# Attention weights turned by TensorE transposes and multiplied with the values in plain float32

## The chip, the cores and the metric

The kernel runs on one core of a Trainium2 chip. What counts is the time of one execution on the device, in microseconds (us): 3889.59 us is the median of three runs of the kernel before (3884.24 to 3891.26).

## The reference

Two blocks, one after the other, over 512 tokens (and 256 context tokens in the first block) of 1024 features. All weights and activations are float32.

Block 1 has two layers. Each projects its input and mixes it in three ways: a Fourier mix, attention with 8 query heads over 2 key and value heads of 64 features, and a gated linear recurrence ("HGRN") of 4 heads. In layer 0 the 256 context tokens have queries of their own, so there 512 queries meet 768 keys, and 256 queries meet 256 keys; in layer 1 only the 512 queries remain. A gated feed-forward part follows each mix.

Block 2 has a layer of feed-forward, causal attention with 8 heads beside a linear recurrent unit, and feed-forward; then one with a gated convolution between two feed-forward parts.

The attention, cut to what matters:

```python
s = einsum('bkgqd,bksd->bkgqs', q, k) * HEAD_DIM ** -0.5
p = softmax(s, axis=-1)                      # over the keys
out = einsum('bkgqs,bksd->bkgqd', p, v)      # weights with the values
```

In block 2 the scores of keys that come after the query are masked first.

## The kernel before

Activations lie with features on the 128 partitions and tokens along the row. A float32 product that has to be exact is made of several products in a rounded float32 form (`float32r`): each operand is split into a high part (a copy, on ScalarE) and a remainder (a subtraction, on VectorE or GpSimd), and `mm3` (L238 to L246) adds high by high, high by remainder and remainder by high in one bank of PSUM. Nearly all of TensorE's work is `mm3`. Small products, such as sums of squares (L295), go to TensorE as unsplit float32.

The phases run in a row: the opening, mix of layer 0, feed-forward, mix of layer 1, feed-forward, feed-forward of block 2, its causal attention ("moba" in the code), and so on. Inside a mix, Python generators for the projections (`dense`), HGRN, Fourier and attention are emitted side by side by `_weave`, by a cost that each step yields; a scheduler of the framework then puts the instructions of each engine in their final order. Each engine works through its own list strictly in that order. PSUM has 8 banks of 512 floats, handed out by `ps()`: the bank that has been free for longest comes next. On-chip memory is handed out likewise from `arena` (float32) and `rarena` (float32r), with a third piece, `room`, lent to one of them.

One head of attention in a mix of block 1 (L947 to L981): for each tile of 128 queries TensorE makes the scores (L959, two banks for 768 keys), VectorE takes their maximum (L535) and scales it (L540), ScalarE makes the exponentials and their sum (L541), VectorE the inverse of the sum (L542), and VectorE in layer 0 or GpSimd in layer 1 a diagonal matrix of it (L544). When the four query tiles are done, TensorE turns the weights for each block of 128 keys by a product with that diagonal, which transposes and normalizes them (L971). The 128 x 512 result is split: high part on ScalarE (L211), remainder on VectorE (L212). Two products with the values follow (L975, L976), one for each part; their stationary operand holds the high part of the values in 64 columns and the remainder in the other 64. `pv_out` (L548) adds the two halves of the result: ScalarE copies one (L550), VectorE adds the other (L551). In block 2 the same steps are at L1425 (scores), L1427 (mask, added by VectorE in PSUM), L1439, L1446 and L1447; there only the keys up to the query are turned.

`bcast_r` (L264) spreads per-token numbers over the partitions: VectorE repeats a column (L268), and a float32 product with the identity turns it (L270). Every root mean square of the kernel goes through it.

## Time and profile before

| | us |
|---|---|
| median of three runs | 3889.59 |
| lowest and highest of them | 3884.24, 3891.26 |
| span of the profiled execution, first to last instruction | 3885.8 |

For the profiled execution the span is the only time given; the median lies 3.8 us above it.

| stretch, us from the start | what runs | length | TensorE busy | VectorE busy | ScalarE busy |
|---|---|---|---|---|---|
| 268 to 510 | attention of layer 0, with HGRN and Fourier | 242 | 203.61 | 182.55 | 120.29 |
| 1318 to 1496 | attention of layer 1, with HGRN and Fourier | 178 | 158.21 | 118.20 | 90.10 |
| 2384 to 2506 | causal attention of block 2, with projections | 122 | 112.72 | 95.01 | 55.92 |
| 600 to 1100 | feed-forward of layer 0 | 500 | 497.74 | 215.90 | 160.99 |

How to read it: over the whole span TensorE is busy 95% of the time, VectorE 51%, ScalarE 35%. A matmul row in the profile lasts from its first column to the end of its drain, so rows of a stream overlap: what a product costs TensorE is the distance from its start to the next start, and TensorE's "busy" holds some time in which it only drains.

### The profile page before, as it was taken

Reading aid. Unit: us, or ns where it says so; the run is one execution under the profiler, and the core shown is the slowest. Engines: PE = TensorE matmul, PEld = TensorE weight load, DVE = VectorE, ACT = ScalarE, POOL = GpSimd, SP = SyncE. Lnnn points to the kernel's source line nnn. Section 1 sums busy time; section 2 is a strip of 40 time slices with the busy share of each in tenths; the row PEclk is TensorE's granted clock in tenths of the full one; section 3 lists DMA queues with packets and bytes.
Section 4 is the critical chain, followed back from the end, with each engine's and each line's share of the span. In section 5 each row is a group of like instructions: output and inputs, shape, how many; then the busy total and the mean of one; then the engine's idle time right before and its main releaser. Section 6 shows DMA issues by size and latency. Waiting matters only on the chain.

```text
span 3885.8 us, 50537 instructions
## 1 busy us (share of the span) xinstructions
PE 3710.8 (95%) x20451; PEld 3210.1 (83%) x20451; DVE 1978.6 (51%) x3637; ACT 1347.7 (35%) x2263; POOL 590.4 (15%) x539
## 2 busy tenths in 40 slices
PE   6998899999999988999999998999999999999998
PEld 5786788888887778888988886798888888888887
DVE  8677756543254765433542457663336334636233
ACT  4233544441232354323332335442224223324222
POOL 3331012540013411000100021120002001111001
PEclk9998999999998999999999999999999999999999
DMA  5222115452202112322132321132223222322222
GB/s 208 66 93 69 37 39 168 157 180 90 63 33 74 39 64 71 105 97 95 61 110 72 117 68 50 60 104 92 76 93 106 96 76 94 102 67 97 98 99 70
DMA packets 95834, 345.12 MB, mean 89 GB/s; under 512 B 10864, under 2 KB 14064, under 8 KB 95600
## 3 DMA queue, kind: packets, MB, share of 16 engines
q1 hardware_dynamic: 95024, 341.37, 26.4%
q8 instruction: 160, 2.62, 0.3%
q14 instruction: 74, 0.61, 0.0%
q10 hardware_dynamic: 576, 0.52, 0.0%
HBM read 334.51 MB, written 4.19 MB: 87 GB/s over the span
## 4 chain that ended last, share of the span: by engine, by line
PE 61%; DVE 5%; issue 1%; ACT 1%; DMA 1%; POOL 1%; SPq 0%; DVEq 0%; POOLq 0%; ACTq 0%
PE psum L244 19%; PE psum L245 18%; PE psum L246 18%; PE psum L971 1%; PE psum L295 1%; DVE rarena L1126 1%; PE psum L830 1%; DVE rarena L231 0%; DVE arena L1171 0%; PE psum L270 0%; PE psum L1425 0%; DMA room<-ab_in 0%; PE psum L1439 0%; PE psum L959 0%; DVE room L535 0%
## 5 line engine op out<-in xcount | busy, mean ns | idle before, releaser
L244 PE MATMUL psum<-rarena,room 128*128 128x512 f32 (+1 forms) x3353 | 1163.0, 348 | 5.9 <-ACT rarena L211 3.2
L245 PE MATMUL psum<-rarena,room 128*128 128x512 f32 (+1 forms) x3297 | 1146.5, 348 | 10.8 <-DVE rarena L1126 9.5
L246 PE MATMUL psum<-rarena,room 128*128 128x512 f32 (+1 forms) x3285 | 1145.9, 349 | 0.8 <-DVE room L231 0.8
L246 PE MATMUL psum<-rarena 128*128 128x512 f32 (+1 forms) x2236 | 782.2, 350 | 12.2 <-DVE rarena L231 11.8
L244 PE MATMUL psum<-rarena 128*128 128x512 f32 (+1 forms) x2168 | 772.6, 357 | 14.0 <-ACT rarena L211 5.8
L245 PE MATMUL psum<-rarena 128*128 128x512 f32 (+1 forms) x2134 | 758.4, 356 | 4.4 <-DVE rarena L1126 2.3
L244 PEld LDWEIGHTS psum<-rarena,room 128*128 128x128 f32 x3353 | 639.9, 191 | 83.3 <-ACT rarena L211 3.3
L245 PEld LDWEIGHTS psum<-rarena,room 128*128 128x128 f32 x3297 | 629.6, 191 | 89.4 <-DVE rarena L1126 12.8
L246 PEld LDWEIGHTS psum<-rarena,room 128*128 128x128 f32 x3285 | 626.8, 191 | 78.6 <-DVE room L231 1.0
L231 DVE TENSOR_TENSOR room<-arena,room 128x1024 fp32r<-128x1024 f32 (+2 forms) x250 | 326.4, 1309 | 523.7 <-PE psum L245 263.5
L229 ACT ACTIVATE room<-arena 128x1024 fp32r<-128x1024 f32 (+2 forms) x290 | 320.2, 1110 | 714.4 <-DMA arena<-gu 217.3
L246 PEld LDWEIGHTS psum<-rarena 128*128 128x128 f32 x2236 | 429.8, 192 | 66.3 <-DVE rarena L231 13.3
L283 POOL TENSOR_TENSOR arena<-arena 128x256 f32<-128x256 f32 x170 | 136.1, 807 | 2291.9 <-ACT arena L281 2217.8
L244 PEld LDWEIGHTS psum<-rarena 128*128 128x128 f32 x2168 | 417.7, 193 | 72.9 <-ACT rarena L211 6.0
L245 PEld LDWEIGHTS psum<-rarena 128*128 128x128 f32 x2134 | 411.5, 193 | 58.5 <-DVE rarena L1126 3.1
L229 ACT ACTIVATE rarena<-arena 128x1024 fp32r<-128x1024 f32 (+2 forms) x138 | 154.6, 1123 | 335.5 <-PE psum L246 101.1
L231 DVE TENSOR_TENSOR rarena<-arena,rarena 128x1024 fp32r<-128x1024 f32 (+2 forms) x98 | 128.9, 1316 | 232.1 <-ACT rarena L229 113.8
L211 ACT ACTIVATE rarena<-arena 128x512 fp32r<-128x512 f32 (+2 forms) x257 | 132.2, 529 | 223.5 <-DVE arena L389 196.8
L212 DVE TENSOR_TENSOR rarena<-arena,rarena 128x512 fp32r<-128x512 f32 (+1 forms) x246 | 151.8, 629 | 97.0 <-ACT rarena L211 96.7
L281 ACT ACTIVATE arena<-arena 128x256 f32<-128x256 f32 (+1 forms) x274 | 106.9, 412 | 240.8 <-DVE arena L1197 119.3
L389 DVE TENSOR_TENSOR arena<-arena,psum 128x512 f32<-128x512 f32 (+1 forms) x170 | 100.9, 598 | 169.5 <-PE psum L246 165.2
L473 POOL TENSOR_TENSOR arena<-arena 128x1024 f32<-128x1024 f32 x48 | 126.3, 2639 | 200.3 <-DMA arena<-w_ada 145.6
(371 smaller groups left out, 3811.2 us busy)
## 6 DMA issues: line engine op xcount, KB each, us to landing
arena<-gu SPq DMA_DIRECT2D x264, 512.0 KB, 3.5
arena<-dn SPq DMA_DIRECT2D x80, 704.0 KB, 4.1
arena<-w_ada SPq DMA_DIRECT2D x60, 512.0 KB, 3.4
room<-w_ada SPq DMA_DIRECT2D x36, 512.0 KB, 4.2
room<-w_in SPq DMA_DIRECT2D x30, 512.0 KB, 3.3
arena<-c_in SPq DMA_DIRECT2D x24, 512.0 KB, 3.2
arena<-dn SPq DMA_DIRECT2D x16, 448.0 KB, 3.4
room<-ab_in SPq DMA_DIRECT2D x14, 512.0 KB, 3.3
```

What stands on the lines that cost most here:

```text
L211: A.activation(h, src, AF.Copy)
L212: eng.tensor_tensor(lo, src, h.bitcast(F32), ALU.subtract)
L229: A.activation(h.r, r.f, AF.Copy)
L231: (G if wlo[1] < wlo[0] else V).tensor_tensor(lo.r, r.f, h.f, ALU.subtract)
L244: PE.matmul(ps, h[:, s], ah, start=k == 0, stop=False)
L245: PE.matmul(ps, h[:, s], al_, start=False, stop=False)
L246: PE.matmul(ps, lo[:, s], ah, start=False, stop=k == nk - 1)
L281: A.activation(sq.f, src, AF.Square)
L283: (V if self.fast else G).tensor_tensor(self.parts[0].f, self.parts[0].f, sq.f, ALU.add)
L295: PE.matmul(pq.f[:, t:t + 1], p.f[:, s], hs[:, 0:1], start=i == 0, stop=i == len(self.parts) - 1)
L389: V.tensor_tensor(s.f, s.f, pu.f, ALU.mult)
L473: G.tensor_tensor(t.f, r.f, sic[q].f, ALU.mult)
```

## The change

- The weights are no longer normalized before the product with the values. `softmax_tile` writes the exponentials and puts their sum into a column of a table that two heads share; the inverse per tile and the diagonal are gone.
- `weighted` turns the weights of a key block by TensorE transposes with the identity, evacuates them with one copy, on ScalarE and VectorE in turn, and multiplies them with the unsplit values in one float32 product. Its stationary operand is 64 columns wide, and it writes the upper or the lower 64 partitions of a bank that both heads share.
- `normed` works once per two heads: one inverse of all their sums, one `bcast_r` per query tile, a copy out of PSUM on ScalarE, a multiplication on VectorE. `pv_out` is gone.
- The values are copied once and no longer split.
- `bcast_r` turns its columns by a transpose and not by a product.
- In block 2 the causal mask is added by a further product (identity by mask), and not by VectorE.
- Two matters of memory: in `mod_cols` the products that nobody reads go to one scratch tile in layer 0, and HGRN's states (`sn`) are placed as long-lived.

Comments were dropped too, so line numbers of the new file differ. What one head does, before and after:

```diff
-            V.reciprocal(rs, sm)
-            d = al(128)
-            pick("dg" + tag).tensor_scalar(d.f, ident, rs, None, op0=ALU.mult)
...
+        def weighted(po, pr, ps_, v, kb, n0, last):
+            pt = ps()
+            for i, (p, o) in enumerate(ps_):
+                PE.transpose(pt.f[:, n0 + i * 128:n0 + i * 128 + 128], p.f[:, o:o + 128], ident)
+            n1 = n0 + len(ps_) * 128
+            t = al(512)
+            evac[0] += 1
+            if evac[0] % 2:
+                A.activation(t.f[:, n0:n1], pt.f[:, n0:n1], AF.Copy)
+            else:
+                V.tensor_copy(t.f[:, n0:n1], pt.f[:, n0:n1])
+            pf_(pt)
+            PE.matmul(po.f[pr, n0:n1], v, t.f[:, n0:n1], start=kb == 0, stop=last)
             fr(t)
+        def normed(dst, po, sums, nt):
+            V.reciprocal(sums[:, :2 * nt], sums[:, :2 * nt])
+            R = ps()
+            for t in range(nt):
+                bcast_r(sums, R.f, t, 2 * t, 2)
+            A.activation(dst, po.f[:, :nt * 128], AF.Copy)
+            V.tensor_tensor(dst, dst, R.f[:, :nt * 128], ALU.mult)
+            pf_(R)
...
-                PE.matmul(ps[:, tb * 128:tb * 128 + 128], rb.f, ident, start=True, stop=True)
+                PE.transpose(ps[:, tb * 128:tb * 128 + 128], rb.f, ident)
...
+                        po, smb = ps(nq), al(64, True)
...
                             for kb in range(nkb):
-                                pt = ps(nq)
-                                for i in range(len(qts)):
-                                    PE.matmul(pt.f[:, i * 128:i * 128 + 128], pn[i].f[:, kb * 128:kb * 128 + 128], dn_[i].f, start=True, stop=True)
-                                ph, pl = alhl(nq)
-                                psplit(ph.r, pl.r, pt.f, nq, f"ps{l}{kb}")
-                                pf_(pt)
-                                PE.matmul(po.f, vs[:, kb, h // 4], ph.r, start=kb == 0, stop=False)
-                                PE.matmul(po.f, vs[:, kb, h // 4], pl.r, start=False, stop=kb == nkb - 1)
-                                fr(ph, pl)
+                                weighted(po, slice(hh * 64, hh * 64 + 64), [(p, kb * 128) for p in pn],
+                                         vs[:, kb, g * 64:g * 64 + 64], kb, 0, kb == nkb - 1)
                                 yield 0.85
-                            fr(pn, dn_)
-                            pv_out(ao.f[hh * 64:hh * 64 + 64, qts[0] * 128:(qts[-1] + 1) * 128], po.f, nq)
-                            pf_(po)
+                            fr(pn)
+                        normed(ao.f[:, qts[0] * 128:(qts[-1] + 1) * 128], po, smb.f, len(qts))
...
-                            dg = sp[:, qt * 128:nk]
-                            V.tensor_tensor(dg, dg, cm.f, ALU.add)
+                            PE.matmul(sp[:, nn - 256:nn], one.r, cm.r[:, c0:c0 + 256], start=False, stop=True)
```

On TensorE, late in the attention of layer 0 where no HGRN and no Fourier run beside it, one head stood in the list before as follows (L959 scores, L971 turns, L975 and L976 products with the values; 128x512 is the result):

```order
L971 MATMUL psum<-room 128x128 x16
L959 MATMUL psum<-rarena 128x512 x2
L975 MATMUL psum<-rarena 128x512
L976 MATMUL psum<-rarena 128x512
L975 MATMUL psum<-rarena 128x512
L959 MATMUL psum<-rarena 128x256 x2
L976 MATMUL psum<-rarena 128x512
L975 MATMUL psum<-rarena 128x512
L976 MATMUL psum<-rarena 128x512
L975 MATMUL psum<-rarena 128x512
```

Now it stands there like this (L978 scores, L551 transposes of the weights, L270 those of `bcast_r`, L560 products with the values, 64 partitions high):

```order
L978 MATMUL psum<-rarena 128x512 x2
L978 MATMUL psum<-rarena 128x256 x2
L978 MATMUL psum<-rarena 128x512 x2
L551 MATMUL psum<-ident,room 128x128 x24
L270 MATMUL psum<-ident,arena 128x128 x2
L270 MATMUL psum<-ident,room 128x128
L560 MATMUL psum<-room,arena 64x512 x2
L978 MATMUL psum<-rarena 128x256 x2
L560 MATMUL psum<-room,arena 64x512
L978 MATMUL psum<-rarena 128x256 x2
L270 MATMUL psum<-ident,arena 128x128
L560 MATMUL psum<-room,arena 64x512 x3
```

All 24 turns of a head's six key blocks now stand in one run behind the last scores of the head, and products 64 high alternate with products 128 high.

On VectorE, at the end of the attention of layer 1, this stood before (L535 and L540 maxima, L542 inverses, L212 remainders, L551 the sum of the halves, L231 remainders of weights for other products):

```order
L542 RECIPROCAL room<-room 128x1 x2
L212 TENSOR_TENSOR rarena<-psum,rarena 128x512 x6
L231 TENSOR_TENSOR rarena<-room,rarena 128x1024
L535 TENSOR_REDUCE room<-psum 128x1 x2
L231 TENSOR_TENSOR rarena<-room,rarena 128x1024
L540 SCALAR_TENSOR_TENSOR room<-room,arena 128x1
L551 TENSOR_TENSOR arena<-psum,room 64x512
L540 SCALAR_TENSOR_TENSOR room<-room,arena 128x1
```

Now there stands (L538 and L543 maxima, L558 evacuations, L567 the inverse for two heads, L268 the columns of `bcast_r`, L572 the multiplication):

```order
L558 COPY room<-psum 128x512 x3
L231 TENSOR_TENSOR rarena<-room,rarena 128x1024
L538 TENSOR_REDUCE arena<-psum 128x1 x2
L543 SCALAR_TENSOR_TENSOR arena<-arena 128x1 x2
L538 TENSOR_REDUCE arena<-psum 128x1 x2
L543 SCALAR_TENSOR_TENSOR arena<-arena 128x1 x2
L231 TENSOR_TENSOR rarena<-room,rarena 128x1024
L567 RECIPROCAL arena<-arena 128x8
L268 COPY arena<-arena 128x128
L268 COPY room<-arena 128x128 x2
L268 COPY arena<-arena 128x128
L558 COPY room<-psum 128x512 x3
```

Six remainders per head have become three copies, and the inverse and its four columns stand once per two heads, ahead of the second head's last copies.

## Rows read from the trace of the kernel before

**Rows 1.** The page: the span, and busy time with its share by engine
```profile
span 3885.8 us, 50537 instructions
PE 3710.8 (95%) x20451; PEld 3210.1 (83%) x20451; DVE 1978.6 (51%) x3637; ACT 1347.7 (35%) x2263; POOL 590.4 (15%) x539
```

**Rows 2.** Stretches: from:to, length, busy of PE, PEld, DVE, ACT, POOL, granted clock, DMA, GB/s
```profile
268.00:510.00 242.00, 203.61 (x1220) 169.50 (x1219) 182.55 (x423) 120.29 (x244) 35.52 (x33) 0.92 0.17 54
1318.00:1496.00 178.00, 158.21 (x935) 132.53 (x934) 118.20 (x242) 90.10 (x172) 44.03 (x60) 0.94 0.15 50
2384.00:2506.00 122.00, 112.72 (x553) 87.30 (x551) 95.01 (x287) 55.92 (x142) 10.77 (x7) 0.97 0.16 57
```

**Rows 3.** Order of time, one head in layer 0: start, us, engine, line, count
```profile
453.48 3.84 PE L971 MATMUL psum<-room 128*128 128x128 f32 x32 [0.74 <-ACT room L541]
455.12 3.05 ACT L211 ACTIVATE rarena<-psum 128x512 fp32r<-128x512 f32 x6 [1.04 <-PE psum L971]
455.75 3.68 DVE L212 TENSOR_TENSOR rarena<-psum,rarena 128x512 fp32r<-128x512 f32 x6 [1.15 <-ACT rarena L211]
463.84 0.68 DVE L551 TENSOR_TENSOR arena<-psum,room 64x512 f32<-64x512 f32 x1
464.58 0.73 PE L959 MATMUL psum<-rarena 128*128 128x512 f32 x2 [1.32 <-DVE arena L551]
469.40 0.96 DVE L535 TENSOR_REDUCE room<-psum 128x1 f32<-128x768 f32 x1 [0.20 <-PE psum L959]
469.71 0.99 ACT L541 ACTIVATE room<-psum,room,arena 128x768 f32<-128x768 f32 x1
482.18 0.67 DVE L551 TENSOR_TENSOR arena<-psum,arena 64x512 f32<-64x512 f32 x1
```

**Rows 4.** Order of time, TensorE, turns by a product
```profile
399.54 0.38 PE L971 MATMUL psum<-room 128*128 128x128 f32 x2
399.76 0.39 PE L971 MATMUL psum<-room,arena 128*128 128x128 f32 x2
```

**Rows 5.** Order of time: weight loads of four transposes; a pair of unsplit 128x512 products
```profile
2475.06 0.46 PEld L557 LDWEIGHTS psum<-ident,room 128*128 128x128 f32 x4
...
2343.30 1.88 PE L1327 MATMUL psum<-room 128*128 128x512 f32 x4
```

**Rows 6.** Order of time, TensorE, block 2: split products and a change of shape
```profile
2471.12 0.39 PE L1446 MATMUL psum<-rarena 128*128 128x512 f32 x1
2471.35 0.40 PE L1447 MATMUL psum<-rarena 128*128 128x512 f32 x1
2471.58 0.33 PE L1446 MATMUL psum<-rarena 128*128 128x384 f32 x1
2471.85 0.62 PE L1425 MATMUL psum<-rarena 64*128 64x256 f32 x3
```

**Rows 7.** Groups on VectorE by shape: line, shapes, count | busy us, mean ns | idle before
```profile
L212 DVE TENSOR_TENSOR rarena<-psum,rarena 128x512 fp32r<-128x512 f32 x126 | 82.0, 685 | 44.2 <-ACT rarena L211 43.7
L544 DVE TENSOR_SCALAR room<-ident,room 128x128 f32<-128x128 f32 x55 | 17.9, 325 | 1.0
L268 DVE COPY arena<-arena 128x128 f32<-128x128 f32 x72 | 14.5, 241 | 1.3
L542 DVE RECIPROCAL room<-room 128x1 f32<-128x1 f32 x84 | 13.3, 158 | 22.2 <-ACT room L541 18.8 <-ACT arena L541 3.0
L551 DVE TENSOR_TENSOR arena<-psum,room 64x512 f32<-64x512 f32 x19 | 12.9, 681 | 4.0 <-ACT room L550 3.6
L707 DVE COPY arena<-psum 128x512 f32<-128x512 f32 x4 | 2.7, 681 | 3.7 <-PE psum L557 3.7
L1427 DVE TENSOR_TENSOR psum<-psum,room 128x128 f32<-128x128 f32 x32 | 9.2, 292 | 4.6 <-PE psum L1425 4.5
```

**Rows 8.** Stretches with their granted clock, columns as in rows 2
```profile
318.00:329.00 11.00, 8.84 (x52) 7.41 (x53) 7.61 (x19) 5.69 (x12) 6.51 (x8) 0.83 0.00 1
329.00:332.00 3.00, 3.00 (x16) 3.00 (x15) 2.13 (x4) 1.17 (x3) 0.20 (x1) 0.50 0.00 0
```

109 lines of the change are left out of this document (47 added, 62 removed).

## The prediction

> **What bounds the kernel now.** I read the page first, then the table of stretches, then the order of time inside one head, then the groups of VectorE by shape. The page shows TensorE busy 95% of a span of 3885.8 us and VectorE 51% [rows 1], so over the whole kernel TensorE is the bound. The change, though, touches three stretches, and those look different [rows 2]: TensorE is busy for 203.61 of 242 us in the attention of layer 0, 158.21 of 178 in layer 1 and 112.72 of 122 in block 2. That leaves 38.4, 19.8 and 9.3 us, together 67.5 us, in which it stands still, and its busy time holds drains besides. VectorE works 182.55, 118.20 and 95.01 us there, 75%, 66% and 78%. No engine is full, so what sets the pace is a chain between engines.
>
> The order of time of one head shows that chain [rows 3]. TensorE turns the 16 last of the 24 weight blocks in one go from 453.48; ScalarE and VectorE split the results from 455.12 and 455.75, VectorE needing 3.68 us for six; the products with the values follow; `pv_out` ends the head with an addition at 463.84; and the next scores, at 464.58, had waited 1.32 us for that addition, since it frees their bank. The next head's addition is at 482.18. So a head in the part of layer 0 with nothing beside it takes 18.3 us.
>
> TensorE's own work in those 18.3 us is less. A product with the diagonal is two instructions, and one follows the next by 0.22 us (399.54, 399.76) [rows 4]. A split 512-wide product takes 0.23 us (2471.12 to 2471.35) [rows 6], so two take 0.46, and 256 columns half of it. A head of layer 0 has scores of four tiles with 768 keys (4 x 2 x 0.35 = 2.8 us) and two with 256 keys (0.5), 28 turns (6.2), and, with the values, six pairs of products of 512 columns and two of 256 (3.2): 12.7 us. The other 5.6 us are waits.
>
> **The change part by part: TensorE.** The trace has each operation but one. Four transposes load their weights in 0.46 us, of which one load is 0.14, so they follow each other by 0.11 us [rows 5]. An unsplit 512-wide product is two instructions; four rows last 1.88 us with 0.59 for the last one, so 0.43 each and 0.86 the product [rows 5]. That one has 128 stationary columns; the new one has 64, which no row shows at this width. Its cost lies between 0.43 (two halves of the array at work side by side) and 0.96 (with a drain each time); I take 0.86, since the list keeps the two heads' products apart. A change of array shape costs a drain: from a 384-wide product to the first with 64 rows it is 0.27 us, where 384 of 512 columns are 0.17 [rows 6], so 0.10 us.
> - Turns: 8 heads x 28 in layer 0, 8 x 24 in layer 1, 8 x 10 in block 2, 496 in all, from 0.22 to 0.11: -54.6 us.
> - Products with the values: 96 of 512 columns, 0.86 in place of 0.46, +38.4; 16 of 256, +3.2; in block 2 1280 unsplit columns per head (2.15 us) for 1408 split ones twice (1.27), +0.88 x 8 = +7.0.
> - `normed`: 56 transposes, +6.2. Mask: 32 products of 256 columns at 0.115, +3.7.
> - Changes of shape: counted in the lists, 180 before and 352 now, 77 more in layer 0, 58 in layer 1, 37 in block 2: 172 x 0.10 = +17.2.
> - Old uses of `bcast_r`: 106 turns, -11.7.
>
> By stretch that is +8.1, +5.7 and +7.4 us, and -11.7 spread over the kernel: TensorE gets 9.5 us more to do, not less.
>
> **VectorE.** Removed: 112 inverses at 0.158 (17.7), 80 diagonals at 0.325 (26.0; layer 1's were GpSimd's), the remainders, 0.685 for 512 columns (85.0 for 96 + 8 + 20 such widths), `pv_out` at 0.681 (19.1), 32 masks at 0.292 (9.3). Added: every other evacuation, 0.681 for 512 columns (42.2), the multiplications (9.5), 56 columns at 0.241 (13.5) [rows 7]. Net -92 us: -41 in layer 0, -20 in layer 1, -31 in block 2. ScalarE keeps half of its copies of 0.51 us (3.05 for six) [rows 3], about -32 us. I count these at nothing by themselves: they lie beside TensorE's 203.61, 158.21 and 112.72 us. They count where the chain runs through them.
>
> **The chain of a head, now.** Layer 0, nothing beside: scores 3.3, 28 transposes 3.1, values 6.0, `normed` 0.3, ten changes of shape 1.0: 13.7 us. New is a wait: all 24 turns stand directly behind the last scores and the first needs all four tiles, so TensorE stands for a maximum (0.96) and the exponentials (0.99) [rows 3] with the scaling and handovers, say 2.4 us. Queued behind it are the next products with the values and the next scores. That gives 16.1 us for 18.3, a gain of 2.2. The split's second step and the wait for `pv_out` before the next scores are gone: `normed` ends a pair of heads, and its columns stand ahead of the copies in VectorE's list, so its transposes are ready when TensorE comes to them. At worst a pair waits for them as long as a head did for the addition, 1.32 us.
>
> Four heads of layer 0 run so; four run beside HGRN and Fourier, whose own work fills part of the waits, and I give them half: 4 x 2.2 + 4 x 1.1 = 13.2. Layer 1 has as many heads, and one takes 178 / 8 = 22 us for 11.5 us of TensorE's work (2.8 scores, 2.6 turns, 5.2 values, 0.2, 0.7), so there is room; the same 13.2. In block 2 TensorE is busy 112.72 of 122 and gets 7.4 us more, against 31 us less on VectorE: 0, between -9 (all its idle time) and +7. Of the 11.7 us from `bcast_r` I take 8: each mean square ends in it with others waiting, but the part inside the waits is lost. Scratch tile and HGRN's placing change no engine's work: 0.
>
> Sum: -13.2 - 13.2 + 0 - 8 = -34.4 us against the profiled span: 3851.4 us. The median lies 3.8 us above the span, so **3855 us**.
>
> **The rivals.**
> 1. More is gained: the lists of ScalarE and VectorE are now so light that the exposed wait is filled, and a head falls to its 13.7 us (4.6 less, beside other work 2.3). For it: TensorE's bound, not VectorE's, is then left in each stretch. Against: the run of 24 turns that waits for four tiles. 2 x 27.6 + 9 + 11.7 = 76: 3814 us.
> 2. Nothing is gained: TensorE's extra 21.2 us in the stretches eat what the chain gives, and the heads beside HGRN follow HGRN's own chain. Only `bcast_r` is left, -12 to +4: about 3885 us.
> 3. Slower, by the clock. The granted clock is 0.92, 0.94 and 0.97 in the three stretches [rows 2], and it falls after short stands: from 318 to 329 us TensorE is busy 8.84 of 11 us, and from 329 to 332 the clock is 0.50, that is 1.2 GHz [rows 8]. If a run of transposes, up to 24 or 2.6 us, works on the clock like a stand, each of the 16 heads of block 1 may bring two more stretches of 3 us at half speed and each of the 8 in block 2 one: 40 x 1.5 = 60 us, so 3855 + 60 = 3915 us. It decides from 23 such stretches on (34.4 / 1.5). For it: the turns by products, 0.22 us of the array's work each [rows 4], go. Against: the unsplit products work it for 0.40 us longer each. The Trainium skill says in "TensorE: Matmul & The Clock Gate", Part 4 (PE-mode transpose), that the full clock does not engage on transposes, which count less as work of the array. By that rule rival 3 is what comes; the runs of transposes in this trace are four long, so no row tells.
> 4. Slower, by banks: the bank of the result is now held through the scores of two heads; if one more pair of score banks is missing and each of the 64 tiles with 768 keys waits for a maximum (0.96), the price is 61 us: 3916 us. Against: the list puts at most two tiles of scores ahead of a run of turns.
> 5. The transposes cost what the products did (0.22): +66 us. Against it is the row of four [rows 5].
>
> **How the numbers follow.** My forecast has 51%, rival 1 12%, rival 2 13%, rival 3 17%, rival 4 5%, rival 5 2%. No change means within 0.2% (7.8 us), about what a measurement of this kernel can tell. Faster: 51 + 12 = 63%; same 13%; slower 24%. The range reaches from rival 1's 3814 to rival 3's 3915 us and leaves out half of each and the two small ones, some 18%. The forecast's own range is 3830 to 3881: the gain in layers 0 and 1 from nothing to double (26 us each way).
>
> **What would show it.** Right: rows of transposes 0.11 us apart and value products 0.86 us apart; heads of 16 us late in layer 0; a stand of 2 to 3 us on TensorE before each run of 24, released by the exponentials; VectorE some 40 us lower in layer 0; a granted clock no lower than 0.92. Wrong: a clock near 0.8 in the attention (rival 3), scores waiting for evacuations (rival 4), or heads that keep their 18 us because the new stand is longer than 4 us.

## The result and the profile after

The changed kernel takes 3945.59 us (median of four runs, 3939.94 to 3947.35) against 3890.1 us for the kernel before, measured beside it: a ratio of 1.015, 95% interval 1.0138 to 1.0163. It is slower by 55 us. The prediction was 3855 us, faster, with a range up to 3915: wrong in sign, and the time is outside the range.

The page of the changed kernel, the span and the busy time by engine, answers to [rows 1]:

```profile
span 3942.6 us, 49128 instructions
PE 3745.4 (95%) x19937; PEld 3142.2 (80%) x19937; DVE 1889.1 (48%) x3353; ACT 1302.4 (33%) x2157; POOL 563.0 (14%) x507
```

VectorE and ScalarE are lighter by 90 and 45 us (92 and 32 were worked out). Nothing of that shows in the time.

To see where the 56.8 us between the two spans arise, I cut both spans at the same events: first scores of layer 0, first sums of squares after its mix, first sums of squares after its feed-forward, first scores of layer 1, first sums of squares after that mix; and first scores of block 2 to the sums of squares after it. The table of stretches (from:to, length, busy of PE, PEld, DVE, ACT, POOL, granted clock, DMA share, GB/s), first of the kernel before:

```profile
271.00:549.00 278.00, 239.61 (x1451) 202.57 (x1449) 192.15 (x435) 127.66 (x258) 42.94 (x42) 0.93 0.16 53
549.00:1116.00 567.00, 562.04 (x3346) 502.06 (x3346) 263.47 (x409) 191.65 (x324) 141.02 (x67) 1.00 0.36 117
1116.00:1322.00 206.00, 191.97 (x1156) 167.68 (x1156) 120.06 (x304) 68.81 (x147) 62.00 (x67) 0.93 0.17 54
1322.00:1527.00 205.00, 183.44 (x1092) 155.15 (x1091) 129.59 (x255) 102.83 (x191) 49.59 (x67) 0.95 0.17 57
2384.00:2535.00 151.00, 140.07 (x719) 111.83 (x718) 104.93 (x296) 70.98 (x168) 16.80 (x15) 0.98 0.17 60
```

The same stretches of the kernel after:

```profile
274.00:573.00 299.00, 253.85 (x1221) 173.98 (x1220) 155.28 (x328) 105.99 (x213) 42.22 (x37) 0.87 0.16 49
573.00:1146.00 573.00, 564.87 (x3348) 504.27 (x3346) 254.28 (x386) 190.35 (x321) 134.56 (x65) 0.99 0.36 116
1146.00:1367.00 221.00, 193.68 (x1132) 167.58 (x1132) 116.22 (x319) 70.71 (x150) 67.82 (x79) 0.91 0.16 51
1367.00:1579.00 212.00, 192.90 (x910) 129.21 (x909) 114.76 (x214) 86.88 (x162) 28.02 (x25) 0.92 0.17 54
2436.00:2591.00 155.00, 151.61 (x696) 107.47 (x695) 78.62 (x170) 62.26 (x136) 17.41 (x16) 0.96 0.19 61
```

A stretch falls into three parts that can be read off such a row. What TensorE is not busy is idle time. Of the length, the missing share of the clock (1 less the granted clock) is time lost at 1.2 GHz, since work there takes twice as long (split products 512 wide follow each other by 0.43 us at 1286 us in the kernel after, and by 0.23 at full clock). The rest is work at full clock (to about 1.5 us in the stretches of 300 us and less, since the clock is given to two digits). This count makes the loss too large where TensorE stands idle at 1.2 GHz, since idle time loses nothing; the last column has that idle time, from the trace's clock records and TensorE's stands.

| stretch | longer by | idle before, after | lost to the clock | work at full clock | idle at 1.2 GHz |
|---|---|---|---|---|---|
| attention of layer 0 | 21 | 38.4, 45.2 | 19.5, 38.9 | 220, 215 | 3.8, 13.6 |
| feed-forward of layer 0 | 6 | 5.0, 8.1 | 0, 6 | 562, 559 | 0.1, 1.0 |
| to the first scores of layer 1 | 15 | 14.0, 27.3 | 14.4, 19.9 | 178, 174 | 3.6, 6.6 |
| attention of layer 1 | 7 | 21.6, 19.1 | 10.3, 17.0 | 173, 176 | 1.5, 3.6 |
| attention of block 2 | 4 | 10.9, 3.4 | 3.0, 6.2 | 137, 145 | 0, 0.6 |

The 4 us that are left lie before the first scores of layer 0 (3) and behind block 2's attention (1). With half of the last column taken out of the loss (half of the time at 1.2 GHz is what work loses there), the clock costs 31 us for 17 in layer 0's attention, 15 for 10 in layer 1's and 6.5 for 3.4 in block 2's, and TensorE's work in the three changes by +1, +3 and +8 us. Over the whole span the same cut gives 22 us more idle time, 29 us more lost to the clock and 6 us more work.

So TensorE has hardly more work than it had; it runs more of it at 1.2 GHz, it waits longer before layer 1, where no attention runs, and the waits of the attention in layers 0 and 1, on which the prediction had put its gain, are as long as ever.

What they are made of did change. Waits of TensorE in layer 0's attention, before (who waited, for whom: us in total, times, longest):

```profile
PE psum L959 <- DVE arena L551: 4.9, 5, 1.6
...
PE psum L971 <- ACT room L541: 3.6, 5, 1.0
PE psum L976 <- DVE rarena L212: 2.3, 3, 1.2
...
PE psum L959 <- ACT room L541: 1.5, 3, 0.6
```

and after:

```profile
PE psum L551 <- ACT room L544: 12.6, 8, 3.6
PE psum L978 <- ACT room L544: 6.1, 4, 2.9
```

The waits for the second step of the split and for `pv_out` are gone. In their place the transposes (L551) and the next scores (L978, their banks) wait for exponentials, 18.7 us where it was 5.1, in fewer and longer stands: of all stands of 2 us or more in this stretch before has 2 (6.9 us together), after 9 (28.6 us).

One head late in layer 0 of the kernel after, on TensorE, as [rows 3] of before:

```profile
449.83 1.11 PE L978 MATMUL psum<-rarena 128*128 128x512 f32 x4 [2.94 <-ACT room L544]
...
452.66 2.19 PE L551 MATMUL psum<-ident,room 128*128 128x128 f32 x12
...
456.97 1.07 PE L560 MATMUL psum<-room,arena 128*64 128x512 f32 x2
457.97 0.50 PE L978 MATMUL psum<-rarena 128*128 128x256 f32 x2
458.40 1.07 PE L560 MATMUL psum<-room,arena 128*64 128x512 f32 x2
459.40 0.50 PE L978 MATMUL psum<-rarena 128*128 128x256 f32 x2
...
489.63 0.47 PE L551 MATMUL psum<-ident,room 128*128 128x128 f32 x1 [2.95 <-ACT room L544]
```

Two halves of a product with the values, 64 columns wide, keep TensorE for 1.00 us until the scores start (456.97 to 457.97), 0.14 more than the 0.86 taken; for a change of shape the prediction had booked 0.10 apart. ScalarE's copy that ends a pair of heads gives the length of a pair:

```profile
477.20 0.60 ACT L571 ACTIVATE arena<-psum 128x512 f32<-128x512 f32 x1 [6.18 <-PE psum L560]
...
516.47 0.60 ACT L571 ACTIVATE arena<-psum 128x512 f32<-128x512 f32 x1 [6.24 <-PE psum L560]
```

39.3 us for two heads, 19.6 a head: not the 16.1 of the prediction, and more than the 18.3 of [rows 3]. What TensorE does in them, first in the head of [rows 3], then in this pair (columns as in the stretches):

```profile
464.00:482.00 18.00, 15.46 (x91) 13.51 (x91) 12.77 (x33) 10.95 (x22) 1.81 (x1) 0.91 0.09 30
```

```profile
477.00:516.00 39.00, 33.26 (x135) 18.41 (x134) 17.05 (x42) 16.14 (x35) 1.80 (x1) 0.91 0.05 15
```

TensorE was idle for 2.5 us of the old head, and is idle for 2.9 us of a new one; it was busy for 15.5 us and is for 16.6, at the same clock.

Last, the longest stand of the stretch before layer 1. Order of time on TensorE, ScalarE and in SP's queue:

```profile
1284.55 0.79 PE L244 MATMUL psum<-rarena 128*128 128x512 f32 x1 [8.03 <-ACT rarena L229]
```

```profile
1283.44 1.06 ACT L229 ACTIVATE rarena<-room 128x1024 fp32r<-128x1024 f32 x1 [9.31 <-DMA rarena<-rarena]
```

```profile
1273.82 6.20 SPq L767 DMA_DIRECT2D rarena<-rarena  x8
```

TensorE stands 8.03 us for the high part of a weight (L229). ScalarE could not write it: the piece of memory it was given was still in use by eight transfers inside that memory (L767), issued over 6.20 us. The transfers lay out the keys of the attention, a step that the change leaves as it was; that it stands in the way of a weight is a matter of who was given which piece of memory, and e8_noscratch below bears that out. The longest stand of the kernel before in this stretch is 3.80 us.

### The profile page after: what moved, and what is told of

It is laid out like the page before. It is cut to its first block, busy times and chain, and to the rows that moved or that the text cites. A ratio compares the mean times of both kernels' runs of the same rounds, so it can differ in the third digit from the quotient of the medians.

```text
span 3942.6 us, 49128 instructions
## 1 busy us (share of the span) xinstructions
PE 3745.4 (95%) x19937; PEld 3142.2 (80%) x19937; DVE 1889.1 (48%) x3353; ACT 1302.4 (33%) x2157; POOL 563.0 (14%) x507
## 5 line engine op out<-in xcount | busy, mean ns | idle before, releaser
L244 PE MATMUL psum<-rarena,room 128*128 128x512 f32 (+1 forms) x3346 | 1163.5, 348 | 14.4 <-ACT rarena L211 11.0
L231 DVE TENSOR_TENSOR room<-arena,room 128x1024 fp32r<-128x1024 f32 (+2 forms) x251 | 326.0, 1303 | 588.7 <-PE psum L245 278.6
L229 ACT ACTIVATE room<-arena 128x1024 fp32r<-128x1024 f32 (+2 forms) x290 | 320.4, 1110 | 697.7 <-DMA arena<-gu 236.4
L229 ACT ACTIVATE rarena<-arena 128x1024 fp32r<-128x1024 f32 (+2 forms) x140 | 157.0, 1122 | 351.9 <-DMA arena<-gu 109.0
L231 DVE TENSOR_TENSOR rarena<-arena,rarena 128x1024 fp32r<-128x1024 f32 (+2 forms) x100 | 135.5, 1355 | 214.6 <-ACT rarena L229 115.3
L212 DVE TENSOR_TENSOR rarena<-arena,rarena 128x256 fp32r<-128x256 f32 (+1 forms) x248 | 146.2, 603 | 93.5 <-ACT rarena L211 93.2
L474 POOL TENSOR_TENSOR arena<-arena 128x1024 f32<-128x1024 f32 x48 | 122.7, 2569 | 196.4 <-DMA arena<-w_ada 139.6
```

Source lines behind the costliest of these rows:

```text
L212: eng.tensor_tensor(lo, src, h.bitcast(F32), ALU.subtract)
L229: A.activation(h.r, r.f, AF.Copy)
L231: (G if wlo[1] < wlo[0] else V).tensor_tensor(lo.r, r.f, h.f, ALU.subtract)
L244: PE.matmul(ps, h[:, s], ah, start=k == 0, stop=False)
L474: G.tensor_tensor(t.f, r.f, sic[q].f, ALU.mult)
```

## The experiments

Two theories at first, about the clock. "Clock": transposes lower TensorE's clock (rival 3). "Stands": the clock falls after TensorE has stood still, whatever it did before. Beside both stood the question which part of the diff costs the time. A ratio below is to the kernel before on the same chip, with its 95% interval.

**e1_products**: the changed kernel, weights turned by a product with the identity.

```diff
-                PE.transpose(pt.f[...], p.f[:, o:o + 128], ident)
+                PE.matmul(pt.f[...], p.f[:, o:o + 128], ident, start=True, stop=True)
```

> The changed kernel, with the 496 turns of the weights made by a float32 product with the identity (0.22 us each) in place of a transpose (0.11 us); all else as changed. TensorE gets 54.6 us more to do. Clock theory (a run of transposes works on the clock like a stand): the stretches at 1.2 GHz in the attention of layer 0, 75 us in the changed kernel and 37 us before, go back to about 40 us, and the time is at or below the changed kernel's 3946 us. Stand theory (the clock falls after TensorE has stood for 2 to 4 us on the exponentials, on memory or on a DMA, whatever the turns are made of): the stretches at 1.2 GHz stay near 75 us and the time rises by 30 to 55 us, to 3975 to 4000 us.

3970.43 us, 1.0212 (1.0196 to 1.0228): 25 us slower than the change. The three attention stretches:

```profile
272.00:587.00 315.00, 274.69 (x1451) 200.09 (x1449) 157.99 (x328) 107.74 (x215) 43.88 (x37) 0.90 0.15 47
1379.00:1604.00 225.00, 208.70 (x1101) 145.61 (x1100) 114.86 (x214) 87.10 (x162) 28.41 (x25) 0.97 0.15 51
2459.00:2616.00 157.00, 156.55 (x777) 115.47 (x777) 81.47 (x170) 63.60 (x139) 18.28 (x16) 0.99 0.18 61
```

In layer 0 the clock is 0.90 against 0.87 with transposes and 0.93 before (65 us at 1.2 GHz, 75 in the change, 37 before): without any transpose of weights most of the lost clock stays lost, as "stands" has it. In layer 1 and block 2 it comes back, to 0.97 and 0.99 from 0.92 and 0.96, as "clock" has it; but TensorE also has 25 and 10 us more work there than in the change. The time lies just below what "stands" expected. This run decides between neither.

**e2_core**: the change without the transposes of `bcast_r`, the scratch tile and the mask as a product. **e3_rest**: the kernel before with these three alone. **e4_wide**: the change with value products 128 columns wide and a bank for each of the two heads.

```diff
 e2_core, against the change
-            PE.transpose(ps[...], rb.f, ident)
+            PE.matmul(ps[...], rb.f, ident, start=True, stop=True)
-            junk = al(1024, True) if len(MODV[l]) == 4 else None
-                            PE.matmul(sp[:, nn - 256:nn], one.r, cm.r[:, c0:c0 + 256], start=False, stop=True)
+                            V.tensor_tensor(dg, dg, cm.f, ALU.add)
 e4_wide, against the change
-            PE.matmul(po.f[pr, n0:n1], v, t.f[:, n0:n1], start=kb == 0, stop=last)
+            PE.matmul(po.f[:, n0:n1], v, t.f[:, n0:n1], start=kb == 0, stop=last)
-                        po, smb = ps(nq), al(64, True)
+                        po, smb = [ps(nq), ps(nq)], al(64, True)
```

> The changed kernel with three edits undone: bcast_r by a product, no scratch tile in mod_cols, the causal mask added by VectorE. Left are the attention itself (transposes, unsplit products, sums per two heads) and the placing of HGRN's states, without which the memory does not suffice. Theory that the attention itself costs the time: 3935 to 3955 us, the loss of about 24 us in layer 0 and the late weights ahead of the attention of layer 1 are there again. Theory that the side edits cost it (bcast_r, scratch tile, mask by changed places in memory and a changed order): 3885 to 3905 us.

> The kernel before with only the side edits: bcast_r by transposes, the scratch tile, the mask as a product; the attention itself as before. Theory that the attention costs the time: 3875 to 3890 us, 106 turns save up to 11.7 us and the mask costs 4. Theory that the side edits cost it: 3910 to 3950 us, with a stand of TensorE of about 8 us on late weights in the projections of layer 1.

> The changed kernel with the value products 128 columns wide (the values of both key heads as the stationary operand, one bank per head, of which half is read; normed copies each head's half by itself). The array's shape no longer changes for them, so some 170 drains of 0.10 us go; ScalarE copies twice as often in normed. Drains on the path: 15 to 20 us faster than the changed kernel, 3925 to 3932 us. Drains beside the waits (stand theory in its strong form): within 5 us of 3946 us.

e2_core 3962.39 us, 1.0197 (1.0178 to 1.0217); e3_rest 3899.42, 1.003 (1.0019 to 1.0042); e4_wide 3963.36, 1.0196 (1.0181 to 1.0212). The new attention, with HGRN's states placed as in the change, costs more than the whole change; the side edits alone cost 12 us although they take work from TensorE; and both together cost less than the sum: a first sign that something decides which none of the steps counts. None of the three came out as expected. e4_wide changes two things at once, in block 2 too; e15_unsplit128 tests the width by itself, in block 1. e3_rest turns no weight by a transpose, and yet its layer 0 has the clock at 0.90, 58 us at 1.2 GHz:

```profile
277.00:561.00 284.00, 250.06 (x1443) 209.38 (x1442) 189.49 (x437) 127.62 (x258) 43.91 (x42) 0.90 0.16 54
```

**e5_split**: before with transposes for the weights and in `bcast_r`, inverse sums once per two heads; values still split, HGRN's states placed as before.

```diff
-                                    PE.matmul(pt.f[...], pn[i].f[:, kb * 128:kb * 128 + 128], dn_[i].f, start=True, stop=True)
+                                    PE.transpose(pt.f[...], pn[i].f[:, kb * 128:kb * 128 + 128], ident)
```

> The kernel before with the weights turned by transposes, the inverse sums once per two heads and the turns of `bcast_r` as transposes; the values stay split, in products 128 high, 0.46 us a pair. TensorE's work falls by 496 x 0.11 = 54.6 and by 11.7 us and rises by 6.2. Theory 'unsplit products' (the loss of the changed kernel lies in value products of 0.95 us and their changes of shape): this kernel keeps about half of the 60 us, 3850 to 3870 us. Theory 'chain' (TensorE's work in the attention is not what sets the pace; the waits for exponentials and for the second step of the split remain): 3880 to 3895 us. Theory 'transposes lower the clock': the stretches at 1.2 GHz in layer 0's attention grow to 70 us and more as in the changed kernel, 3900 to 3930 us.

3871.03 us, 0.9951 (0.9935 to 0.9968): faster than before by 16 to 19 us, next to the range that the theory of the unsplit products gave (3850 to 3870), but only after a loss: it is 35 us ahead at the end of layer 1's mix and gives 22 back in block 2, where its clock is 0.80 (173 us for 151). Why the clock is so low there is not shown.

```profile
2348.00:2521.00 173.00, 156.35 (x665) 119.37 (x664) 102.50 (x254) 70.96 (x168) 16.78 (x15) 0.80 0.16 52
```

So transposes do gain in block 1.

**e6_const**: the change, with the transposes of block 1 reading the values, so that they need not wait for exponentials.

```diff
-                                weighted(po, ..., [(p, kb * 128) for p in pn],
+                                weighted(po, ..., [(self.vs, i * 128) for i in range(len(pn))],
```

> The changed kernel, in which the transposes of block 1's attention read the values in place of the weights, so that they need not wait for the exponentials; exponentials, sums and everything else are worked out as before, and the result of the attention isn't the reference's. Theory 'stands' (TensorE waits for the exponentials ahead of its runs of transposes, and the clock falls after that): some 16 us of waiting in layer 0 and half of that in layer 1 go, and 30 to 40 us of the stretches at 1.2 GHz with them: 3900 to 3915 us against 3946. Theory 'unsplit products': the waits move to the copies and banks, 3935 to 3945 us. If transposes themselves lowered the clock, the stretches at 1.2 GHz would stay at 75 us in layer 0, with 3930 us.

3924.08 us, 1.0092 (1.0077 to 1.0107): 21 us less than the change, where "stands" expected 31 to 46. In layer 0 idle time is 39.5 for 45.2 us and the clock 0.90 for 0.87; TensorE ran into other waits (eight stands of 2 us or more, nine in the change).

```profile
275.00:561.00 286.00, 246.52 (x1226) 170.01 (x1225) 155.08 (x328) 107.32 (x215) 44.76 (x37) 0.90 0.17 52
```

**e7_probe**: before with runs of turns that nobody uses, put into two feed-forward parts that run at full clock: 24 transposes a run in the one, 12 products with the identity in the other, 19 runs each.

```diff
+                            for i in range(24):
+                                if self.name == "ffn1":
+                                    PE.transpose(pt.f[:, o], self.act[i % 8][0].f[:, 0:128], ident)
+                                elif i % 2:
+                                    PE.matmul(pt.f[:, o], self.act[i % 8][0].f[:, 0:128], ident, start=True, stop=True)
```

> The kernel before with work added that nobody uses: in the feed-forward of layer 1 19 runs of 24 transposes, and in the first feed-forward of block 2 19 runs of 12 products with the identity, each run among split products that keep TensorE at full speed. At full clock either adds 19 x 2.6 = 50 us, together 100: 3987 us. Theory 'transposes lower the clock': after each run of transposes a stretch at 1.2 GHz, so that the first feed-forward gets 50 + 19 x 1.7 = 82 us or more longer, the second 50; 4020 us and more. Theory 'stands': both get 50 us longer and the granted clock of both stays at 0.99 or above.

3993.02 us, 1.027 (1.0255 to 1.0286). The two feed-forward parts, in before and then here:

```profile
1527.00:1895.00 368.00, 364.31 (x1851) 313.48 (x1851) 138.54 (x198) 109.44 (x148) 6.68 (x8) 0.99 0.28 95
1895.00:2267.00 372.00, 371.09 (x1934) 320.10 (x1933) 153.69 (x237) 116.89 (x170) 17.44 (x22) 1.00 0.27 88
```

```profile
1527.00:1945.00 418.00, 414.31 (x2306) 361.96 (x2305) 140.24 (x216) 108.83 (x148) 6.73 (x8) 0.99 0.25 82
1945.00:2367.00 422.00, 422.00 (x2391) 370.75 (x2390) 155.85 (x256) 118.94 (x170) 17.91 (x22) 1.00 0.24 79
```

```profile
1607.03 2.78 PE L422 MATMUL psum<-ident,rarena 128*128 128x128 f32 x24
```

```profile
2027.09 2.84 PE L424 MATMUL psum<-ident,rarena 128*128 128x128 f32 x24
```

Both are 50 us longer, 19 runs of 2.6 us, at the clock of before (a product is two instructions, so 12 make 24 in the row). A run of 24 transposes among products that keep TensorE busy costs what its instructions cost and nothing of the clock. So transposes by themselves do not lower it; what they do in the attention, where TensorE also stands idle, this run does not test.

**e8_noscratch**: the change without its scratch tile; no engine's work changes.

```diff
-            junk = al(1024, True) if len(MODV[l]) == 4 else None
+            junk = None
```

> The changed kernel without its scratch tile: the products of `mod_cols` that nobody reads go where they went before; no engine's work changes. By the prediction's step (the place of a tile changes no engine's work and costs nothing) 3945 us within 4. Theory 'memory' (who gets which stretch of memory decides when weights are loaded and in which order the scheduler puts the phases): the stand of 8 us in the projections of layer 1 goes or moves, and the time differs by 8 us or more, to either side.

3929.43 us, 1.0109 (1.0094 to 1.0124): 16 us less than the change. The stretch before layer 1 takes 206 us again, without the stand of 8 us; layer 0's feed-forward takes 17 more instead, and the opening 8. What is left of the gain lies in the attention: 10 us less in layer 0, 3 in layer 1, 8 in block 2. "Memory" holds: one tile moves nearly every stretch.

**e9_mix** and **e10_mix2**: block 1 of e5_split, with block 2's attention of the kernel before, and of the changed one.

```diff
 e9_mix, block 2, against e5_split
-                                PE.transpose(pt.f[...], pn[qt].f[:, q0:q0 + 128], ident)
+                                PE.matmul(pt.f[...], pn[qt].f[:, q0:q0 + 128], dn_[qt].f, start=True, stop=True)
 e10_mix2, block 2, against e5_split
-                            PE.matmul(po.f[:, n0:], vr[:, kb, hh], ph.r[:, n0:], start=kb == 0, stop=False)
-                            PE.matmul(po.f[:, n0:], vr[:, kb, hh], pl.r[:, n0:], start=False, stop=kb == 3)
+                            weighted(po, pr, [(pn[qt], q0) for qt in range(kb, 4)], vt[...], kb, q0, kb == 3)
```

> Block 1 as in e5_split (transposes, split values, inverse sums once per two heads), block 2's attention as in the kernel before. e5_split was 35.1 us ahead of before when the mean squares after layer 1's mix began (1492.1 against 1527.2 us), and lost 22.6 us between the first scores of block 2 and the next mean squares (173.5 against 150.9 us), with 75 us at 1.2 GHz there. Theory 'each stretch for itself' (what a stretch loses is due to its own order of work): that loss goes, 3871 - 22.6 = 3848 us, 3842 to 3856. Theory 'given back' (what the attention gains is lost again later, whatever stands there): 3865 to 3875 us.

> Block 1 as in e5_split, block 2's attention as in the changed kernel (unsplit values 64 columns wide, mask as a product), whose stretch took 154.7 us against 150.9 before. Theory 'each stretch for itself': 3871 - 173.5 + 154.7 = 3852 us, 3845 to 3860. Theory 'given back': 3865 to 3880 us.

3859.74 us, 0.9925 (0.9909 to 0.9941), and 3851.46 us, 0.9905 (0.9882 to 0.9928). e9_mix lies between the theories: the loss in block 2 went (154 us for 173), but layer 1 got 4 us longer on the way. e10_mix2 is the fastest of all, 36 us faster than before, and came out as "each stretch for itself" had it. Its attention of layers 0 and 1:

```profile
275.00:539.00 264.00, 224.45 (x1251) 181.89 (x1252) 180.78 (x380) 126.91 (x257) 46.24 (x42) 0.89 0.17 56
...
1310.00:1495.00 185.00, 161.91 (x910) 134.28 (x910) 131.51 (x246) 102.53 (x192) 28.65 (x35) 0.93 0.19 62
```

Idle 39.6 and 23.1 us, as in before. Work at full clock is 195 and 149 us for 220 and 173: all that the turns were counted to save. Layer 1 is 20 us shorter for it, layer 0 only 14, since 10 of its 25 go to the clock (29 us lost for 19.5).

**e12_twice**: e5_split with each pair of value products of block 1 made twice.

```diff
+                                for again in range(2):
-                                PE.matmul(po.f, vs[:, kb, h // 4], ph.r, start=kb == 0, stop=False)
+                                    PE.matmul(po.f, vs[:, kb, h // 4], ph.r, start=kb + again == 0, stop=False)
```

> e5_split with each pair of value products of block 1 made twice into the same bank, so that the attention's result is twice the right one. It adds 8 heads x (6 x 0.46 + 2 x 0.23) = 25.8 us of TensorE's work in layer 0 and 8 x 6 x 0.46 = 22.1 in layer 1, 47.9 us, no change of array shape, no copy and no wait. Theory 'TensorE's work passes through' (the stands of the attention stay what they are, and work added to TensorE adds to the time): 3871 + 48 = 3919 us, 3908 to 3926. Theory 'chain' (waits between engines set the pace and TensorE has 38 us of room in layer 0 and 20 in layer 1): 3871 to 3885 us.

3901.58 us, 1.0035 (1.0024 to 1.0045): 30 of the 48 us came through, between the theories. Layer 1 got 21 us longer for 22 us of work. Layer 0 got 7 longer for 26, and not because idle time was filled (35.9 us, 38.8 in e5_split): its clock rose from 0.89 to 0.95, which gave back 15.

```profile
273.00:544.00 271.00, 235.06 (x1377) 193.01 (x1374) 185.45 (x379) 126.25 (x257) 45.89 (x42) 0.95 0.17 55
```

**e13_bcast**: before with transposes in `bcast_r` alone.

```diff
-            PE.matmul(ps[:, tb * 128:tb * 128 + 128], rb.f, ident, start=True, stop=True)
+            PE.transpose(ps[:, tb * 128:tb * 128 + 128], rb.f, ident)
```

> The kernel before with nothing changed but `bcast_r`, which turns its columns by a transpose: 106 turns of 0.11 in place of 0.22 us, 11.7 us of TensorE's work, all of it where a mean square is waited for. The prediction's step: 8 us less, 3879 us (3875 to 3883). Theory 'memory and order' (the scheduler puts the phases in another order once a duration changes, and that costs or gains more than the step itself): 3887 or more, or under 3872.

3881.06 us, 0.9981 (0.997 to 0.9991): 7 us less. The step's 8 us hold.

**e14_unsplit64, e15_unsplit128, e17_sn**: e10_mix2 with HGRN's states long-lived (e17_sn, nothing else), and on top of that unsplit values in block 1, 64 or 128 columns wide, with a bank for each head.

```diff
 e17_sn, against e10_mix2
-                        sn = al(128)
+                        sn = al(128, True)
 e14_unsplit64 and e15_unsplit128, against e17_sn
-                                PE.matmul(po.f, vs[:, kb, h // 4], ph.r, start=kb == 0, stop=False)
-                                PE.matmul(po.f, vs[:, kb, h // 4], pl.r, start=False, stop=kb == nkb - 1)
+                                weighted(po, slice(hh * 64, hh * 64 + 64), [...], vs[:, kb, j // 2 * 64:j // 2 * 64 + 64], ...)
+                                weighted(po, slice(0, 128), [...], vs[:, kb], ...)
```

> e10_mix2 with unsplit values in block 1 too, in products 64 columns wide, each head with a bank of its own that it gives back at its end, heads one after the other as in e10_mix2, the sums normalized per two heads as there; HGRN's states long-lived. With e8_noscratch (3929 us), which keeps one bank through two heads, it has all but the place of the bank and the order of a pair's heads in common; from e10_mix2 (3851 us) it differs in block 1's value products, 96 x 0.49 + 16 x 0.25 = 51 us more of TensorE's work, and their copies. Theory 'work of the products': 3851 + 51 = 3902 us, 3895 to 3910, and the shared bank and the order of heads have cost the other 27 us. Theory 'everything is in the unsplit form' (its copies and its runs of 24 turns bring the stands and the half clock): 3920 to 3935 us. Theory 'part of the work is hidden', as in e12_twice, where 30 of 48 us came through: 3880 to 3890 us.

> e14_unsplit64 with value products 128 columns wide, of which half is used: 0.86 in place of 0.95 us and no change of array shape. If the changes of shape cost time, 112 x 0.09 = 10 us less than e14_unsplit64, and up to 20 with the change back. e4_wide, which held two banks per pair of heads, came out 17 us slower than the changed kernel; if the second bank was the reason, this one, which holds a single bank for one head, is faster than e14_unsplit64. If wide products are slower for another reason (more stretches at 1.2 GHz), it is slower than e14_unsplit64 by 10 us or more.

> e10_mix2 with HGRN's states placed as long-lived and nothing else: no engine's work changes. By the prediction's step (placing costs nothing): 3851 us within 4. Theory 'memory and order', by which e8_noscratch without its scratch tile was 16 us faster: 3859 us or more, or under 3843. It is also the control for e14_unsplit64, which has its states placed so.

e14_unsplit64 3908.49 us, 1.0052 (1.0037 to 1.0067); e15_unsplit128 3879.27, 0.9982 (0.9972 to 0.9991); e17_sn 3897.71, 1.0031 (1.0021 to 1.004). The third was the surprise: 46 us for the place of some small tiles. 21 of them arise in layer 0's feed-forward, which has neither attention nor HGRN. It stands here from the end of its first sums of squares on, in e10_mix2 and then in e17_sn:

```profile
571.00:1105.00 534.00, 532.07 (x3094) 472.80 (x3095) 238.47 (x336) 174.87 (x285) 135.36 (x61) 1.00 0.38 125
```

```profile
583.00:1140.00 557.00, 538.76 (x3101) 477.60 (x3100) 248.78 (x339) 176.62 (x285) 134.48 (x60) 0.98 0.37 119
```

SP's queue, ScalarE and TensorE in e17_sn show one of the stands. Loads for layer 1's modulation (`w_ada`) keep the queue for 14.81 us, since they wait for memory that ScalarE still uses (L474, 12.9 us in two waits); the feed-forward's own weights (`gu`) are issued behind them at 705.83, ScalarE waits for these to make their high part (L229), and TensorE stands 5.91 us for it:

```profile
682.38 14.81 SPq L466 DMA_DIRECT2D arena<-w_ada  x4
697.29 5.26 SPq L228 DMA_DIRECT2D arena<-dn  x2
...
705.83 0.33 SPq L228 DMA_DIRECT2D arena<-gu  x1
```

```profile
710.04 1.06 ACT L229 ACTIVATE room<-arena 128x1024 fp32r<-128x1024 f32 x1 [5.04 <-DMA arena<-gu]
```

```profile
711.15 0.58 PE L244 MATMUL psum<-rarena,room 128*128 128x256 f32 x1 [5.91 <-ACT room L229]
```

The two others, 128 and then 64 columns wide, in the attention of layers 0 and 1:

```profile
279.00:557.00 278.00, 237.02 (x1246) 182.59 (x1247) 157.41 (x331) 113.00 (x226) 43.23 (x42) 0.88 0.17 53
1322.00:1523.00 201.00, 181.92 (x909) 135.16 (x908) 115.32 (x214) 90.36 (x166) 28.93 (x28) 0.92 0.18 57
```

```profile
277.00:568.00 291.00, 246.48 (x1244) 171.18 (x1241) 156.29 (x330) 112.51 (x226) 44.09 (x42) 0.90 0.16 51
1338.00:1549.00 211.00, 193.86 (x910) 126.81 (x909) 114.05 (x214) 89.26 (x166) 28.57 (x27) 0.92 0.17 55
```

Work at full clock, split to 128 to 64 columns: 195, 204, 217 us in layer 0 and 149, 166, 177 in layer 1. Of the 29 us between the last two kernels 23 lie in these stretches. So the changes of array shape do cost, and the width by itself is a gain. In e4_wide too TensorE has some 11 and 8 us less work in layers 0 and 1 than in the change; its loss there is idle time (53 us for 45, 30 for 19), and block 2 is 8 us longer. Whether the second bank or the memory makes that is not shown.

**e18_before_sn, e19_states, e20_best**: HGRN's states long-lived in the kernel before; in layer 0 alone in e8_noscratch and in e15_unsplit128.

```diff
-                        sn = al(128)
+                        sn = al(128, True)         # e18_before_sn
+                        sn = al(128, l == 0)       # e19_states, e20_best
```

> The kernel before with HGRN's states placed as long-lived, and nothing else: no engine's work changes. By the prediction's step (placing changes no engine's work and costs nothing): 3886 us within 4. Theory 'memory' (the same edit made e10_mix2 46 us slower in e17_sn: loads of weights wait for memory in SP's queue, with other loads behind them, and TensorE stands for them in the feed-forward and the opening): 3900 to 3935 us.

> The changed kernel without its scratch tile, and with HGRN's states long-lived in layer 0 alone; in layer 1 they are placed as before. Against e8_noscratch (3929 us) no engine's work changes. Prediction's step: 3929 us. Theory 'memory': at least 8 us away from that, and if the states' place is what the changed kernel pays for, 3890 to 3915 us.

> e15_unsplit128 (transposes, unsplit values in products 128 wide in block 1, a bank for each head, block 2 as in the changed kernel) with HGRN's states long-lived in layer 0 alone. e15_unsplit128 took 3879 us, 18 less than e17_sn, whose values are split. Prediction's step: 3879 us. Theory 'memory': 3835 to 3870 us, and if it comes under 3851 us, unsplit products were never what made the changed kernel slower.

e18_before_sn 3904.18 us, 1.0058 (1.0041 to 1.0075), 19 us slower by the medians and 22 by the ratio; e19_states 3936.73, 1.0137 (1.0122 to 1.0153), 7 slower than e8_noscratch; e20_best 3887.32, 1.0001 (0.9992 to 1.001), 8 slower than e15_unsplit128. So the placing costs 19 us in the kernel before and 46 in e10_mix2, and taking half of it back costs 7 and 8 more: an expectation that failed in its sign. Each place of these tiles gives another schedule, and none is good by itself. What the place of the states costs in the changed kernel itself is not shown: no run of it has them as before in both layers.

## Why the prediction was wrong

**A ladder of measured kernels.** From before to the change, by their ratios, times 3886 us: states long-lived +22 (e18_before_sn); on top of that transposes (of weights and in `bcast_r`), inverse sums per two heads, unsplit values (128 wide in block 1, 64 in block 2), mask product -30 (e15_unsplit128); 64 columns instead of 128 +27 (e14_unsplit64); one bank for two heads, their order and another place for the sums +22 (e8_noscratch); scratch tile +16 (the change): +57 us. The fourth rung isn't the bank's in the attention: layer 0's feed-forward has 18 us of idle time in e8_noscratch, as in e17_sn, and the attention of both layers is no longer than in e14_unsplit64 (290 and 209 for 291 and 211 us, first scores to sums of squares). So three rungs, some 60 us, are mostly memory and the order that follows from it (for the fourth this is argued from e17_sn and not tested), and one is the shape of the products. A gain of about the forecast's size stands there as one rung, but that is luck: in it layer 0's attention stays at 278 us, and layer 1's and block 2's get 6 us shorter each. Since the price of a placing differs by kernel, each rung is uncertain by some 20 us (an estimate from the 19 and 46 us of the states' place); the third is backed by its own stretches.

**The step that failed first** is "The other 5.6 us are waits", and with it "a gain of 2.2" for a head, the -13.2 us in layer 0 and again in layer 1. The 5.6 us were a difference: the head's 18.3 us less TensorE's work added up. In the trace TensorE is idle for 2.5 us of that head; the rest of the difference is time in which it is busy, 1.6 us of it lost at 1.2 GHz (0.91 of 18 us). The new stand was sized well: 2.9 us idle in a new head, where 2.4 were allowed. So a head's waits went from 2.5 to 2.9 us, and not from 5.6 to 2.4, and TensorE's own time in it rose by 1.2, about the 1.0 that was counted.

The stretches say the same: each wait that went was replaced. Idle time in layer 0's attention is 38 us before and 45 after, and 34 to 45 us in all other kernels but e4_wide (53), for TensorE's work between 195 and 242 us; in layer 1 it is 22 and 19. What moved the time there was TensorE's work and the clock. By the work alone, with the idle time as it is, the three stretches would have been forecast at +21 us on the prediction's own count, and not at -26; they got 32 us longer, 12 by work and 23 by the clock, with 3 less idle. In block 2 the forecast (0, between -9 and +7) held at +4, and there the idle time did give way to work, from 11 to 3 us.

Against the forecast of -34 us for the span the 57 us are off by 91: some 35 in layer 0's attention, 20 in layer 1's, 4 in block 2's, and the rest outside the attention, where -8 had been booked and 25 came.

**The second is "Scratch tile and HGRN's placing change no engine's work: 0."** The first half of the sentence is true and the conclusion isn't. The scratch tile cost 16 us in this kernel, the placing 19 and 46 us in two others. The mechanism is in the trace: a tile's place decides which earlier user a load or a split waits for, SP's queue is in order, and what stands behind waits too.

**TensorE's sum was about right.** It was +9.5 us for the kernel, and 6 were measured. 24 transposes take 2.6 us, 0.11 each, so rival 5 fell. Value products take 1.00 us alone and 0.86 more for each further one in a run (470.54 to 472.40, two of them), near the upper bound (0.96) where they stand alone. Work in the three stretches changed by +1, +3 and +8 us (idle time at 1.2 GHz left out) where +8.1, +5.7 and +7.4 were counted. What the transposes save, 25 and 24 us in block 1 (e10_mix2), the unsplit products 64 wide take back, 22 and 28 (e14_unsplit64 against e10_mix2). The `bcast_r` step (8 us, measured 7) held. VectorE's and ScalarE's 135 us less were counted at nothing, and nothing of them shows in the time.

**Rival 3 saw the place; its cause is neither shown nor ruled out there.** The clock did fall, to 0.87 in layer 0, and by the corrected count that is 14 us there, 6 in layer 1 and 3 in block 2. But e7_probe shows runs of 24 transposes at an unchanged clock. The Trainium skill's "TensorE: Matmul & The Clock Gate", Part 4 (PE-mode transpose), says the full clock does not engage for transposes; here, among products, it stayed engaged, and the measurement decides. In the attention the runs do not agree. Layer 0 has 34 to 44 us at 1.2 GHz in four kernels that turn the weights by products (before, e7_probe, e13_bcast, e18_before_sn) and 58 to 75 us in thirteen that turn them by transposes, as the rival has it; but e3_rest and e1_products have 58 and 65 us with products, and e12_twice, with transposes and more work, has 27. Stands do not settle it either. In the changed kernel each of the nine stands of over 2 us is followed by a stretch at 1.2 GHz or lies in one, and e6_const, which shortens them, raises the clock to 0.90. Yet e3_rest has its 58 us with a single such stand, and e5_split and e12_twice have four each, with 0.89 against 0.95. What sets the clock, and so the cause of 29 of the 57 us (23 of them in the attention), stays open.

**Rival 4** (banks): scores do wait for banks, 6.1 us, a tenth of its price.

**The range** leaves out half of 12 and of 17% with the 5 and the 2, so 21 or 22% by the prediction's own chances, and not 18.

## What to carry to other kernels

Read the idle time of a stretch, and of one head in it, from the profile; the length less the work that one can add up is not idle time. Where it comes from many short waits between engines, do not book a gain for shortening one link before looking for what waits next: in layers 0 and 1 it stayed nearly constant, in block 2 it gave way to work. When tiles come from a shared pool and loads go through a queue in order, an edit that only moves a tile is an edit of the schedule: price it by building the kernel with that edit alone. And split a change into its parts before taking it whole: transposes with split values and the new block 2 (e10_mix2) gave 0.9905 of the time, the same change with narrower products and other places 1.015.

## What was not expected of the hardware

Changes between products 128 and 64 columns wide add up: widening the products took 24 us of work out of two layers although it computes twice as much. The traces have 202 changes of shape there in e14_unsplit64 and 58 in e15_unsplit128, so 0.17 us for each, where the prediction took 0.10. 26 us of products added to a stretch at a granted clock of 0.89 made it only 7 us longer, since the clock rose to 0.95. And 19 runs of 24 transposes, 2.6 us each, left the clock of a feed-forward part where it was (0.99).
